# A two-layer hybrid decoder trunk: gate and up columns of its FFNs by seven half products per pair

## The chip, the cores and the metric

One program on one core of a Trainium2 chip. The metric is the device time of the program in microseconds (us). The kernel before took 2765.47 us, the median of three runs (2765.41 to 2768.8).

## The reference

The input x has 512 positions of 1024 features; everything is float32. Each of two layers runs an FFN, a token mixer (a gated DeltaNet and a dilated attention side by side) and a second FFN, each on a normalised and modulated copy of the residual:

```python
def modulate(x, shift, scale):
    return x * (1.0 + scale[:, None, :]) + shift[:, None, :]
def swiglu(x, w_gate, w_up, w_down):
    return (jax.nn.silu(x @ w_gate) * (x @ w_up)) @ w_down
for l in range(DEPTH):
    mod = c_act @ ada_w[l] + ada_b[l]
    (sh1, sc1, gt1, sh2, sc2, gt2, sh3, sc3, gt3) = jnp.split(mod, N_ADA, axis=-1)
    f = swiglu(modulate(rmsnorm(h, ln_ffn1[l]), sh1, sc1), ffn1_wg[l], ffn1_wu[l], ffn1_wd[l])
    h = h + MACARON_WEIGHT * gt1[:, None, :] * f
    u = modulate(rmsnorm(h, ln_mix[l]), sh2, sc2)
    m = hybrid_mixer(u, w_in[l], conv_w[l], a_log[l], dt_bias[l], dn_norm[l], w_a[l], w_b[l], w_o[l])
    h = h + gt2[:, None, :] * m
    f = swiglu(modulate(rmsnorm(h, ln_ffn2[l]), sh3, sc3), ffn2_wg[l], ffn2_wu[l], ffn2_wd[l])
    h = h + MACARON_WEIGHT * gt3[:, None, :] * f
return rmsnorm(h, final_norm)
```

The gate and up matrices are 1024 x 2816, the down matrix is 2816 x 1024. The change bears on `x @ w_gate` and `x @ w_up`, and on when `c_act @ ada_w` is computed.

## The kernel before, in words

The residual lies in SBUF as eight tiles `h` of 128 features x 512 positions. A product in full precision is made of three passes in a faster format (fp32r): each operand is split into a rounded high part and the rest, and high x high, low x high and high x low are summed in one PSUM bank. For a weight tile of 128 x 512 (four blocks of 128 x 128) the split is one copy on ACT (`wh`) and one subtraction on DVE (`wl`).

A gate or up matrix has 22 column blocks of 128. `dense` (line 298) makes one: 8 blocks along the 1024 features, 3 passes, so 24 matmuls of 128 x 512, each with its own 128 x 128 weights, into one bank. ACT then takes tanh of the gate bank, DVE forms the gated product with the up bank (`g`, `ay`), and `split` (line 739) halves it into `ah` and `al` for the down product. `ffn_order` (line 40) sets the order: the columns of a chunk of the 2816 inner features (`CHUNKS`, 8, 8 and 6 blocks), one ahead, and then the eight down columns over that chunk, whose banks DVE adds into `h`.

Every engine's queue is in the order in which this code is written; a wait in a queue holds all that stands behind it. Weights come from a list of `units`: `w_load` (line 242) issues the load on SP, `w_split` (line 254) the split, and `w_get` (line 277) sees to it that the split stands three units ahead of the one that PE is about to use:

```python
n = st["use"]
while st["split"] <= min(n + ahead, len(units) - 1):
    w_split()
```

The modulation vector is made on DVE, row block by row block, as 288 multiply-and-sum steps of 128 x 512 (`ada_step`, line 342; the tile is `ad`). They are dealt out by `tick`, which `mm_list` (line 288) calls after every third matmul: `ada["rate"]` says how many steps a tick issues, 0.42 in the FFNs until the last chunk. So all of layer 0 is made in its first FFN, and layer 1 in the second FFN of layer 0. GpSimd (POOL) is hardly used in an FFN.

At the end of each stage `tail` (line 481) finishes the last four columns in halves of 256 positions, makes the new normalised input `us` (high and low parts), and begins the first four weight units of the next stage, which for an FFN are gate and up of its first two blocks. `start` (line 633) does the same for the first FFN with eight units, four blocks.

## Time and profile before

| | |
|---|---|
| Median of three runs | 2765.47 us |
| Profiled execution: its own time | 2765.34 us |
| Profiled execution: span | 2763.6 us |
| PE busy | 2721.1 us, 98% |
| DVE busy | 1622.8 us, 59% |
| ACT busy | 1030.8 us, 37% |
| POOL busy | 496.8 us, 18% |
| Mean DMA rate | 126 GB/s |

The span is what the profiler recorded of one execution, from the first instruction to the last; the time of that execution is 1.7 us longer, and it is within 0.2 us of the median. The busy time of PE counts the matmuls with their modelled ends, which overlap, so the rate of PE is better read from the distance between starts. An average over the span hides that the stages differ: POOL's 18% lie nearly all in the two mixers and in the first 60 us.

### The profile page before, as it was taken

To read this page: it belongs to the slowest core of one execution; us is meant where nothing else is said; L and a number is where in the kernel's file an instruction comes from. 1 tells how busy PE (TensorE), PEld (TensorE's weight loads), DVE (VectorE), ACT (ScalarE), POOL (GpSimd) and SP (SyncE) were. 2 spreads that over 40 slices of the span, in tenths; PEclk is the share of its full clock that TensorE was granted. 3 is DMA by queue.
4 is the path that set the end of the run, shared out by engine and by line. 5 is a ranking of instruction groups with operands and counts; after the bars stand their busy time and mean duration, and the time that the engine had idled before them with its cause. 6 is when DMAs were issued, how large, how long until landed. Compare 5 with 4: busy or idle time off the path is not lost.

```text
span 2763.6 us, 39483 instructions
## 1 busy us (share of the span) xinstructions
PE 2721.1 (98%) x14812; PEld 2286.7 (83%) x14812; DVE 1622.8 (59%) x3325; ACT 1030.8 (37%) x2032; POOL 496.8 (18%) x965
## 2 busy tenths in 40 slices
PE   6999999999999999999999999999999999999998
PEld 4888888878888898888898888888788888988887
DVE  8877368666645467776454344776665454643435
ACT  4323235555533333222342222545554333432322
POOL 4000015353440000000010000254445100100001
PEclk9999999999999999999999999999999999999999
DMA  7776323442332337875323332324323333333332
GB/s 250 262 258 204 88 83 108 121 131 68 102 92 92 120 102 251 264 254 171 113 77 99 93 98 86 123 84 127 96 61 110 90 99 123 99 100 98 99 93 68
DMA packets 153391, 349.35 MB, mean 126 GB/s; under 512 B 41584, under 2 KB 44400, under 8 KB 153200
## 3 DMA queue, kind: packets, MB, share of 16 engines
q1 hardware_dynamic: 150640, 338.45, 39.4%
q0 software_dynamic: 2560, 8.39, 0.9%
q8 instruction: 116, 1.90, 0.3%
q14 instruction: 75, 0.61, 0.1%
HBM read 325.80 MB, written 11.53 MB: 122 GB/s over the span
## 4 chain that ended last, share of the span: by engine, by line
PE 93%; DVE 3%; DMA 1%; ACT 1%; issue 1%; SPq 1%; DVEq 0%; ACTq 0%
PE mm L117 80%; PE tl L117 4%; PE as L117 1%; PE ob L117 1%; PE pw L117 1%; PE pq L117 1%; PE po L117 1%; DVE wl L117 1%; PE aT L117 1%; DMA wr<-in_w_in_dram 1%; PE pm L117 1%; DVE sn L117 0%; DVE cy L117 0%; PE pt L117 0%; SPq L128 0%
## 5 line engine op out<-in xcount | busy, mean ns | idle before, releaser
L117 PE MATMUL mm<-uh,wh 128*128 128x512 f32 (+1 forms) x2608 | 680.9, 384 | 11.8 <-ACT uh L117 11.8
L117 PE MATMUL mm<-uh,wl 128*128 128x512 f32 (+1 forms) x2608 | 681.8, 382 | 0.0
L117 DVE TENSOR_TENSOR wl<-wr,wh 128x512 fp32r<-128x512 f32 (+1 forms) x904 | 597.4, 705 | 142.5 <-ACT wh L117 141.5
L117 PE MATMUL mm<-ul,wh 128*128 128x512 f32 (+1 forms) x2608 | 632.5, 380 | 1.6 <-DVE ul L117 1.6
L117 ACT ACTIVATE wh<-wr 128x512 fp32r<-128x512 f32 (+1 forms) x904 | 501.5, 609 | 253.6 <-DMA wr<-in_w_gu_dram 129.5
L117 PEld LDWEIGHTS mm<-uh,wh 128*128 128x128 f32 x2608 | 483.7, 189 | 104.0 <-ACT uh L117 16.8
L117 PEld LDWEIGHTS mm<-uh,wl 128*128 128x128 f32 x2608 | 487.1, 189 | 86.8 <-issue 0.7
L117 PEld LDWEIGHTS mm<-ul,wh 128*128 128x128 f32 x2608 | 466.6, 188 | 87.8 <-DVE ul L117 2.3
L117 POOL TENSOR_SCALAR y<-y,G,mod 128x256 f32<-128x256 f32 (+1 forms) x88 | 63.9, 728 | 1215.1 <-DVE y L117 1186.5
L117 ACT ACTIVATE ah<-ay 128x512 fp32r<-128x512 f32 x88 | 55.6, 632 | 380.6 <-DVE ay L117 380.6
L117 DVE SCALAR_TENSOR_TENSOR ad<-ad,ca 128x512 f32<-128x512 f32 x272 | 173.7, 689 | 0.0
L117 DVE SCALAR_TENSOR_TENSOR h<-mm,gt,h 128x512 f32<-128x512 f32 x88 | 65.2, 750 | 181.9 <-PE mm L117 181.9
L117 ACT ACTIVATE t<-mm 128x512 f32<-128x512 f32 x88 | 52.4, 595 | 315.8 <-PE mm L117 315.8
L117 DVE SCALAR_TENSOR_TENSOR g<-t,mm 128x512 f32<-128x512 f32 x88 | 60.4, 686 | 169.2 <-ACT t L117 169.2
L117 DVE TENSOR_TENSOR ay<-g,mm 128x512 f32<-128x512 f32 x88 | 60.4, 687 | 166.6 <-PE mm L117 165.6
L117 PE MATMUL mm<-ah,wl 128*128 128x512 f32 x608 | 152.8, 389 | 0.0
L117 PE MATMUL mm<-al,wh 128*128 128x512 f32 x608 | 152.7, 389 | 0.0
L117 PE MATMUL mm<-ah,wh 128*128 128x512 f32 x608 | 152.7, 389 | 0.0
L117 PEld LDWEIGHTS mm<-al,wh 128*128 128x128 f32 x608 | 114.1, 188 | 23.7
L117 PEld LDWEIGHTS mm<-ah,wl 128*128 128x128 f32 x608 | 114.1, 188 | 23.7
L117 PEld LDWEIGHTS mm<-ah,wh 128*128 128x128 f32 x608 | 114.1, 188 | 23.7
L117 DVE SCALAR_TENSOR_TENSOR cy<-mm,cw,cy 128x511 f32<-128x511 f32 x144 | 107.0, 746 | 7.0 <-ACT cy L117 3.6
(258 smaller groups left out, 2909.9 us busy)
## 6 DMA issues: line engine op xcount, KB each, us to landing
wr<-in_w_gu_dram SPq DMA_DIRECT2D x176, 512.0 KB, 3.7
ad<-in_ada_w_dram SPq DMA_DIRECT2D x288, 256.0 KB, 4.7
wr<-in_w_in_dram SPq DMA_DIRECT2D x132, 512.0 KB, 4.0
wr<-in_w_dn_dram SPq DMA_DIRECT2D x64, 512.0 KB, 3.6
wr<-in_w_dn_dram SPq DMA_DIRECT2D x32, 384.0 KB, 3.1
wr<-in_w_a_dram SPq DMA_DIRECT2D x16, 512.0 KB, 3.7
wr<-in_w_o_dram SPq DMA_DIRECT2D x16, 512.0 KB, 3.7
al<-in_alibi_dram SPq DMA_DIRECT2D x24, 256.0 KB, 3.2
```

Of the source, the lines that this page charges most:

```text
L117: return fn(*args, **kw)
```

## The change

From the first blocks on (four in the first FFN, two in the others), the gate and up columns are made in pairs. For a pair of column blocks the weights form a 2 x 2 matrix (two column blocks by two halves of the 1024 features, each quarter 128 x 512 in SBUF), and the input one of two halves of the features by two halves of the positions. `dense_pair` computes the 2 x 2 product by Strassen's way in Winograd's form: seven products of a quarter of weights (or a sum of quarters) and a quarter of the input (or a sum). Each product is 4 blocks x 3 passes, 12 matmuls of 128 x 256. In what follows a **round** is the seven products for one pair of blocks of either gate or up. There are 9 pairs in the first FFN and 10 in each of the others, so 78 rounds, and each stands where two `dense` calls stood, 48 matmuls of 128 x 512.

The products accumulate in three banks X, Y and Z. After each one, ACT copies the bank (products 0, 1, 2 and 6) or DVE adds it (3, 4 and 5) into the SBUF tiles `c1` and `c2`; X is written by products 0, 2, 4 and 6, so each of these follows the reading of the one before. Tanh and the gated product then read `c1` and `c2` from SBUF.

The four weight sums of a round are made on GpSimd (`w_sums`, tiles `ws0` to `ws3`, 128 x 512 each), and all seven quarters are split on ACT and DVE: seven splits a round where four were. The sums of the input are made once per FFN at the end of `tail` and `start` (`halves_sums`): 16 sums of 128 x 256, half on GpSimd and half on DVE, and 8 splits of 128 x 512.

Further: the split of weights stands 7 products (1.75 units) ahead of PE in an FFN; raw weights come as pieces of 256 KB out of the common pool of 84 buffers; there are four chunks, of 6, 6, 4 and 6 blocks; and the modulation steps run at 0.13 per tick, a tick being six matmuls in a round, with stops that leave 48 steps to each of the first three FFNs, 16 to the last, and 48 to each mixer (0.18 per tick, from the product that follows the attention).

```diff
-NBIG = 78
-CHUNKS = ((0, 8), (8, 16), (16, 22))
+NBIG = 84
+AHEAD = 1.75
+CHUNKS = ((0, 6), (6, 12), (12, 16), (16, 22))
...
-def ffn_order():
-    seq = []
-    gu = list(range(FF))
-    nxt = 0
+def ffn_order(first):
+    seq = [("gu", i) for i in range(first)]
+    nxt = first
     for ci, (lo, hi) in enumerate(CHUNKS):
-        ahead = min(hi + 1, FF)
-        while nxt < ahead:
-            seq.append(("gu", gu[nxt]))
-            nxt += 1
+        while nxt < min(hi + 1, FF):
+            seq.append(("pair", nxt))
+            nxt += 2
         seq.append(("down", ci))
     return seq
+def first_gu(l, f):
+    return 4 if (l, f) == (0, 0) else 2
...
+                elif kind == "pair":
+                    for gu in range(2):
+                        for j in (i, i + 1):
+                            units.append((("pair", l, f, j, gu), w_gu[l, f, j, gu], 8))
...
+    jobs = []
+    for n, u in enumerate(units):
+        if u[0][0] != "pair":
+            jobs.append((n, None))
+        elif u[0][3] % 2 == 0:
+            jobs += [(n, j) for j in range(7)]
+    st = {"load": 0, "split": 0, "use": 0, "ahead": 3, "lead": 0, "raw": 4}
...
+            raws[n] = []
+            for k0 in range(0, nk, 4):
+                m = min(4, nk - k0)
+                raws[n].append(big("wr", (128, m, 128)))
+                load(out=raws[n][-1], in_=src[:, k0:k0 + m])
         st["load"] += 1
...
+    def halves(r):
+        wh, wl = big("wh", (128, r.shape[1], 128), F32R), big("wl", (128, r.shape[1], 128), F32R)
+        A.activation(out=wh, in_=r, func=AF.Copy)
+        V.tensor_tensor(out=wl, in0=r, in1=wh.bitcast(F32), op=OP.subtract)
+        return wh, wl
+    def w_sums(n):
+        while st["load"] <= n + 1:
+            w_load()
+        (a11, a12), (a21, a22) = (raws[i] for i in (n, n + 1))
+        s1, s2, s3, s4 = (big(f"ws{i}", (128, 4, 128)) for i in range(4))
+        P.tensor_tensor(out=s1, in0=a21, in1=a22, op=OP.add)
+        P.tensor_tensor(out=s2, in0=s1, in1=a11, op=OP.subtract)
+        P.tensor_tensor(out=s3, in0=a11, in1=a21, op=OP.subtract)
+        P.tensor_tensor(out=s4, in0=a12, in1=s2, op=OP.subtract)
+        sums[n] = [s1, s2, s3, s4]
...
+        for n_, j_ in jobs[st["split"]:st["split"] + 4]:
+            if j_ == 0 and n_ not in sums:
+                w_sums(n_)
+        if j is not None:
+            if n not in sums:
+                w_sums(n)
+            s = sums[n]
+            src = (raws[n][0], s[0], s[1], raws[n][1], s[2], s[3], raws[n + 1][1])[j]
+            wh, wl = halves(src)
+            splits[n, j] = [(wh[:, k, :], wl[:, k, :]) for k in range(4)]
+            if j == 6:
+                raws.pop(n), raws.pop(n + 1), sums.pop(n)
+                w_fill()
...
+    def w_ahead(lead):
+        while st["split"] < len(jobs) and st["lead"] < lead:
+            w_split()
...
+        st["lead"] -= weight(job)
+        w_ahead(4 * ahead)
...
+    def dense_pair(keys, us, ts):
+        X, Y, Z = bank("mX"), bank("mY"), bank("mZ")
+        c1, c2 = big("c1"), big("c2")
+        lo, hi = HALF
+        def b(k0, sl):
+            return [(us[k][0][:, sl], us[k][1][:, sl]) for k in range(k0, k0 + 4)]
+        def copy(out, ps):
+            A.activation(out=out, in_=ps[:, lo], func=AF.Copy)
+        def add(out, ps):
+            V.tensor_tensor(out=out, in0=ps[:, lo], in1=out, op=OP.add)
+        for j, (ps, x, first, fn, out) in enumerate((
+                (X, b(0, lo), True, copy, c1[:, lo]), (Z, ts[0], True, copy, c2[:, hi]),
+                (X, ts[1], False, copy, c1[:, hi]), (Y, b(4, lo), True, add, c1[:, lo]),
+                (X, ts[2], False, add, c2[:, hi]), (Z, b(4, hi), False, add, c1[:, hi]),
+                (X, ts[3], False, copy, c2[:, lo]))):
+            w = w_get(keys[0], part=j)
+            lst = passes(w, x, range(4), lo)
+            mm_list([(ps[:, lo], a_, b_, first and i == 0, i == len(lst) - 1)
+                     for i, (a_, b_) in enumerate(lst)], 2 * Q)
+            fn(out, ps)
+        return c1, c2
...
+    def halves_sums(ys):
+        lo, hi = HALF
+        h12 = dnp.tile([128, 4, 2, 256], F32R, name=nm("th"), tag="MT")
+        l12 = dnp.tile([128, 4, 2, 256], F32R, name=nm("tl"), tag="W")
+        h34 = [dnp.tile([128, 2, 2, 256], F32R, name=nm("th"), tag=t_) for t_ in ("bt", "R")]
+        ts = [[None] * 4 for _ in range(4)]
+        for k in range(4):
+            E = (P, V)[k % 2]
+            a, b = big("ta", (128, 2, 256)), big("tb", (128, 2, 256))
+            y0, y1 = ys[k], ys[k + 4]
+            E.tensor_tensor(out=a[:, 0, :], in0=y0[:, hi], in1=y0[:, lo], op=OP.subtract)
+            E.tensor_tensor(out=a[:, 1, :], in0=y1[:, hi], in1=a[:, 0, :], op=OP.subtract)
+            E.tensor_tensor(out=b[:, 0, :], in0=y1[:, hi], in1=y0[:, hi], op=OP.subtract)
+            E.tensor_tensor(out=b[:, 1, :], in0=y1[:, lo], in1=a[:, 1, :], op=OP.subtract)
+            l34 = big("tl", (128, 2, 256), F32R)
+            for q, (t, th, tl) in enumerate(((a, h12[:, k], l12[:, k]), (b, h34[k // 2][:, k % 2], l34))):
+                A.activation(out=th, in_=t, func=AF.Copy)
+                V.tensor_tensor(out=tl, in0=t, in1=th.bitcast(F32), op=OP.subtract)
+                for i in range(2):
+                    ts[2 * q + i][k] = (th[:, i, :], tl[:, i, :])
+        return ts
...
+        w_ahead(12 if any(narrow) else 4)
+        ts = None if any(narrow) else halves_sums(yt)
...
+        w_ahead(4)
+        return us, pss, halves_sums(ys)
...
-        st["ahead"] = 3
-        ada["rate"] = 0.42
-        ada["stop"] = 144 if (l, f) == (0, 0) else len(ada_seq)
-        if f == 1 and ada["pos"] < ada["stop"]:
+        st.update(ahead=AHEAD, raw=4)
+        ada.update(rate=0.13, stop=min(len(ada_seq), 144 * l + 96 * f + 80))
...
+            elif kind == "pair":
+                g2s = dense_pair([("pair", l, f, j, 0) for j in (i, i + 1)], us, ts)
+                for c_ in g2s:
+                    t = big("t")
+                    A.activation(out=t, in_=c_, func=AF.Tanh, scale=0.5)
+                    V.scalar_tensor_tensor(out=c_, in0=t, scalar=1.0, in1=c_, op0=OP.add, op1=OP.mult)
+                ups = dense_pair([("pair", l, f, j, 1) for j in (i, i + 1)], us, ts)
+                for j, (c_, y) in enumerate(zip(g2s, ups)):
+                    V.tensor_tensor(out=y, in0=c_, in1=y, op=OP.mult)
+                    act[i + j] = split(y, "a")
...
-        st["ahead"] = 2
+        st.update(ahead=2, raw=3)
...
+        c_load()
+        c_silu()
+        ada.update(rate=0.18, stop=144 * l + 128)
...
```

Three places show how the instructions stand. The first is DVE's queue in the gate and up columns of the first FFN, before: `wl` is a weight split, `ad` a modulation step, `g`, `ay` and `al` the gated product and its low part, `mm` a PSUM bank.

```order
L117 TENSOR_TENSOR ay_939<-g_222_893,mm_905 128x512
L117 TENSOR_TENSOR al_942<-ay_939,ah_941 128x512
L117 TENSOR_TENSOR wl_946<-wr_903,wh_945 128x512
L117 TENSOR_TENSOR wl_950<-wr_903,wh_949 128x512
L117 SCALAR_TENSOR_TENSOR ad_915,acc_92<-ad_915,ca_108 128x512
L117 SCALAR_TENSOR_TENSOR ad_924,acc_92<-ad_924,ca_106 128x512
L117 SCALAR_TENSOR_TENSOR ad_933,acc_92<-ad_933,ca_108 128x512
L117 SCALAR_TENSOR_TENSOR g_245_991<-t_989,mm_955 128x512
L117 TENSOR_TENSOR wl_994<-wr_953,wh_993 128x512
L117 TENSOR_TENSOR wl_998<-wr_953,wh_997 128x512
L117 SCALAR_TENSOR_TENSOR ad_962,acc_92<-ad_962,ca_106 128x512
```

And DVE's queue now, in the second half of an up round of the first pair (`c_263` and `c_264` are `c1` and `c2` of the round, `mX`, `mY` and `mZ` its banks, `ws` a sum by GpSimd, `wr` a loaded quarter):

```order
L122 TENSOR_TENSOR wl_1063<-wr_839,wh_1062 128x512
L122 TENSOR_TENSOR c_263_998<-mY_996,c_263_998 128x256
L122 TENSOR_TENSOR wl_1080<-ws_240_898,wh_1079 128x512
L122 SCALAR_TENSOR_TENSOR ad_924,acc_92<-ad_924,ca_106 128x512
L122 TENSOR_TENSOR c_264_999<-mX_995,c_264_999 128x256
L122 TENSOR_TENSOR wl_1100<-ws_241_899,wh_1099 128x512
L122 TENSOR_TENSOR c_263_998<-mZ_997,c_263_998 128x256
L122 TENSOR_TENSOR wl_1117<-wr_843,wh_1116 128x512
L122 TENSOR_TENSOR c_263_998<-c_220_823,c_263_998 128x512
L122 TENSOR_TENSOR al_1143<-c_263_998,ah_1142 128x512
L122 TENSOR_TENSOR c_264_999<-c_221_824,c_264_999 128x512
L122 TENSOR_TENSOR al_1148<-c_264_999,ah_1147 128x512
```

Where two splits stood to one column, seven stand to a round, and three additions out of the banks stand between them; each addition waits for its product, and what follows it in the queue waits with it.

The second is ACT's queue, before, over one block:

```order
L117 ACTIVATE wh_2269<-wr_2226 128x512
L117 ACTIVATE wh_2273<-wr_2226 128x512
L117 ACTIVATE ah_2315<-ay_2313 128x512
L117 ACTIVATE wh_2319<-wr_2277 128x512
L117 ACTIVATE wh_2323<-wr_2277 128x512
L117 ACTIVATE t_2361<-mm_2329 128x512
L117 ACTIVATE wh_2365<-wr_2327 128x512
L117 ACTIVATE wh_2369<-wr_2327 128x512
L117 ACTIVATE ah_2404<-ay_2402 128x512
```

And now, from the end of an up round (`c_264<-mX_995`, the copy of its last product) into the next gate round, whose first copies are `c_296<-mX_1151` and `c_297<-mZ_1153`:

```order
L122 ACTIVATE wh_1099<-ws_241_899 128x512
L122 ACTIVATE wh_1116<-wr_843 128x512
L122 ACTIVATE c_264_999<-mX_995 128x256
L122 ACTIVATE ah_1142<-c_263_998 128x512
L122 ACTIVATE ah_1147<-c_264_999 128x512
L122 ACTIVATE wh_1156<-wr_968 128x512
L122 ACTIVATE c_296_1154<-mX_1151 128x256
L122 ACTIVATE wh_1173<-ws_272_1054 128x512
L122 ACTIVATE c_297_1155<-mZ_1153 128x256
L122 ACTIVATE wh_1193<-ws_273_1055 128x512
L122 ACTIVATE c_296_1154<-mX_1151 128x256
```

The copy of the next round's first product stands behind the two `ah`, which wait for DVE, and behind a weight split.

The third is GpSimd's queue, where nothing stood in this stage: the end of the input's sums, and the weight sums of two rounds.

```order
L122 TENSOR_TENSOR ta_758<-y_325 128x256
L122 TENSOR_TENSOR ta_758<-y_615,ta_758 128x256
L122 TENSOR_TENSOR tb_759<-y_615,y_325 128x256
L122 TENSOR_TENSOR tb_759<-y_615,ta_758 128x256
L122 TENSOR_TENSOR ws_238_896<-wr_841,wr_843 128x512
L122 TENSOR_TENSOR ws_239_897<-ws_238_896,wr_837 128x512
L122 TENSOR_TENSOR ws_240_898<-wr_837,wr_841 128x512
L122 TENSOR_TENSOR ws_241_899<-wr_839,ws_239_897 128x512
L122 TENSOR_TENSOR ws_272_1054<-wr_972,wr_974 128x512
L122 TENSOR_TENSOR ws_273_1055<-ws_272_1054,wr_968 128x512
```

They wait for no product of PE; each waits for its loaded quarters, for the sum before it and for a free buffer.

## Rows read from the trace of the kernel before

**Rows 1.** The page of the whole span: busy time by engine, and the granted clock.
```profile
span 2763.6 us, 39483 instructions
...
PE 2721.1 (98%) x14812; PEld 2286.7 (83%) x14812; DVE 1622.8 (59%) x3325; ACT 1030.8 (37%) x2032; POOL 496.8 (18%) x965
...
PEclk9999999999999999999999999999999999999999
```

**Rows 2.** The page, chain that ended last: shares of the span by engine.
```profile
PE 93%; DVE 3%; DMA 1%; ACT 1%; issue 1%; SPq 1%; DVEq 0%; ACTq 0%
```

**Rows 3.** Windows: busy us (x instructions) of PE, PEld, DVE, ACT, POOL; clock, DMA share, GB/s.
```profile
200.00:378.00 178.00, 178.00 (x787) 147.39 (x786) 97.08 (x200) 52.01 (x97) 0.00 (x0) 1.00 0.46 144
...
800.00:1000.00 200.00, 200.00 (x1182) 167.01 (x1181) 97.98 (x172) 68.97 (x130) 9.19 (x26) 1.00 0.37 114
```

**Rows 4.** Timeline of PE in a gate/up column: start us, us, operation, xcount.
```profile
205.08 1.98 PE L117 MATMUL mm<-uh,wh 128*128 128x512 f32 x8
...
212.34 1.98 PE L117 MATMUL mm<-uh,wl 128*128 128x512 f32 x8
```

**Rows 5.** Timeline of PE in a tail, where products have 256 columns.
```profile
1004.91 1.12 PE L117 MATMUL tl<-mh,wl 128*128 128x256 f32 x8
...
1010.67 1.12 PE L117 MATMUL tl<-mh,wl 128*128 128x256 f32 x8
```

**Rows 6.** Timeline of DVE in the same gate/up column as rows 4.
```profile
206.52 1.29 DVE L117 TENSOR_TENSOR wl<-wr,wh 128x512 fp32r<-128x512 f32 x2
...
208.33 0.69 DVE L117 SCALAR_TENSOR_TENSOR ad<-ad,ca 128x512 f32<-128x512 f32 x1
...
208.94 0.69 DVE L117 SCALAR_TENSOR_TENSOR ad<-ad,ca 128x512 f32<-128x512 f32 x1
```

**Rows 7.** Groups of DVE, 205 to 370 us, an FFN: busy us, mean ns | idle before, releaser.
```profile
L117 DVE TENSOR_TENSOR wl<-wr,wh 128x512 fp32r<-128x512 f32 x58 | 37.5, 684 | 0.0
L117 DVE SCALAR_TENSOR_TENSOR ad<-ad,ca 128x512 f32<-128x512 f32 x36 | 22.9, 685 | 0.0
L117 DVE TENSOR_TENSOR al<-ay,ah 128x512 fp32r<-128x512 f32 x11 | 7.6, 693 | 7.9 <-ACT ah L117 7.9
L117 DVE SCALAR_TENSOR_TENSOR h<-mm,gt,h 128x512 f32<-128x512 f32 x8 | 6.0, 750 | 26.6 <-PE mm L117 26.6
```

**Rows 8.** DVE on 256 elements out of PSUM (tile tl): min/median/max ns.
```profile
L117 DVE SCALAR_TENSOR_TENSOR h<-tl,gt,h x48: 475/484/485, 384.0 to 2751.7; 128x256 f32<-128x256 f32 x48
```

**Rows 9.** Groups of ACT, whole span.
```profile
L117 ACT ACTIVATE wh<-wr 128x512 fp32r<-128x512 f32 x856 | 488.1, 620 | 253.6 <-DMA wr<-in_w_gu_dram 129.5 <-DMA wr<-in_w_dn_dram 58.8 <-DMA wr<-in_w_b_dram 25.6
...
L117 ACT ACTIVATE ah<-ay 128x512 fp32r<-128x512 f32 x88 | 55.6, 632 | 380.6 <-DVE ay L117 380.6
L117 ACT ACTIVATE t<-mm 128x512 f32<-128x512 f32 x88 | 52.4, 595 | 315.8 <-PE mm L117 315.8
...
L117 ACT ACTIVATE PT<-aT 128x256 f32<-128x256 f32 x24 | 8.8, 366 | 0.2
```

**Rows 10.** Timeline of DVE and POOL side by side, both out of SBUF, at the start.
```profile
42.98 2.99 POOL L117 TENSOR_TENSOR ad<-ad,ca 128x512 f32<-128x512 f32 x2
43.09 1.73 DVE L117 TENSOR_TENSOR ul<-y,uh 128x512 fp32r<-128x512 f32 x1 [0.35 <-POOL y L117]
...
44.74 2.38 DVE L117 TENSOR_TENSOR wl<-wr,wh 128x512 fp32r<-128x512 f32 x2
...
47.04 0.68 DVE L117 SCALAR_TENSOR_TENSOR ad<-ad,ca 128x512 f32<-128x512 f32 x1
```

**Rows 11.** The same POOL operation over the run (tile ad): min/median/max ns.
```profile
L117 POOL TENSOR_TENSOR ad<-ad,ca x16: 1258/1666/1742, 13.2 to 64.4; 128x512 f32<-128x512 f32 x16
```

**Rows 12.** Timeline of DVE out of PSUM beside POOL, in the mixer.
```profile
464.78 1.49 POOL L117 TENSOR_TENSOR gu<-cm,gl 128x512 fp32r<-128x512 f32 x1
...
465.29 2.31 DVE L117 SCALAR_TENSOR_TENSOR cy<-mm,cw,cy 128x511 f32<-128x511 f32 x3
...
470.17 1.53 DVE L117 SCALAR_TENSOR_TENSOR cy<-mm,cw,cy 128x511 f32<-128x511 f32 x2
```

More of the change, by code (lines that the diff above doesn't have):

```diff
@@ L228, in trunk @@
                     units.append((("o", l, o), w_o[l, o], 8))
-            for kind, i in ffn_order():
+            for kind, i in ffn_order(first_gu(l, f)):
                 if kind == "gu":
@@ L237, in trunk @@
                                       w_dn[l, f, o][:, lo * 128:hi * 128], hi - lo))
-    NRAW = 3
-    st = {"load": 0, "split": 0, "use": 0, "ahead": 3}
-    raws, splits = {}, {}
+    jobs = []
[5 more added lines that the diff above has]
+    st = {"load": 0, "split": 0, "use": 0, "ahead": 3, "lead": 0, "raw": 4}
+    raws, splits, sums = {}, {}, {}
     def w_load():
@@ new lines, in w_load, with weight @@
+        st["load"] += 1
+    def weight(job):
+        return 4 if job[1] is None else 1
+    def halves(r):
[13 more added lines that the diff above has]
+        sums[n] = [s1, s2, s3, s4]
@@ L254, in w_split @@
     def w_split(load=True):
-        n = st["split"]
+        n, j = jobs[st["split"]]
+        st["split"] += 1
+        st["lead"] += weight((n, j))
         while st["load"] <= n:
             w_load()
+        for n_, j_ in jobs[st["split"]:st["split"] + 4]:
[11 more added lines that the diff above has]
+                w_fill()
+            return
@@ L260, in w_split, with w_fill, w_get, mm_list @@
         if units[n][0][0] == "in" and units[n][0][2] == T_BA:
-            splits[n] = r
-            st["split"] += 1
-            w_load()
-            return
-        parts = []
-        for k0 in range(0, nk, 4):
-            m = min(4, nk - k0)
-            wh, wl = big("wh", (128, m, 128), F32R), big("wl", (128, m, 128), F32R)
-            A.activation(out=wh, in_=r[:, k0:k0 + m], func=AF.Copy)
-            V.tensor_tensor(out=wl, in0=r[:, k0:k0 + m], in1=wh.bitcast(F32), op=OP.subtract)
-            parts.append((wh, wl))
-        splits[n] = [(parts[k // 4][0][:, k % 4, :], parts[k // 4][1][:, k % 4, :]) for k in range(nk)]
-        st["split"] += 1
-        if load:
-            w_load()
-    def w_get(key, ahead=None):
-        n = st["use"]
+            splits[n, None] = r
+            w_fill()
+            return
+        parts = [halves(x) for x in r]
+        splits[n, None] = [(parts[k // 4][0][:, k % 4, :], parts[k // 4][1][:, k % 4, :]) for k in range(nk)]
+        if load:
+            w_fill()
+    def w_fill():
+        while len(raws) < st["raw"] and st["load"] < len(units):
+            w_load()
+    def w_ahead(lead):
+        while st["split"] < len(jobs) and st["lead"] < lead:
+            w_split()
+    def w_get(key, ahead=None, part=None):
+        job = jobs[st["use"]]
         ahead = st["ahead"] if ahead is None else ahead
-        assert units[n][0] == key, (units[n][0], key)
-        while st["split"] <= min(n + ahead, len(units) - 1):
+        assert units[job[0]][0] == key and job[1] == part, (units[job[0]][0], key, job, part)
+        while st["split"] <= st["use"]:
+            if ahead < 0:
+                break
             w_split()
         st["use"] += 1
-        return splits.pop(n)
+        st["lead"] -= weight(job)
+        w_ahead(4 * ahead)
+        return splits.pop(job)
     Q = 3
-    def mm_list(lst):
+    def mm_list(lst, q=Q):
         for i, (ps, lhsT, rhs, start, stop) in enumerate(lst):
-            T.matmul(ps, lhsT=lhsT, rhs=rhs, start=start, stop=stop)
-            if i % Q == Q - 1:
+            T.matmul(ps, lhsT=lhsT, rhs=rhs, start=start, stop=stop, skip_group_check=q != Q)
+            if i % q == q - 1:
                 tick()
@@ L572, in tail @@
         ys = {}
+        yt = [big("y") for _ in range(NF)] if not any(narrow) else [None] * NF
         def first(k, hf):
@@ L625, in tail @@
         low()
-        while st["split"] < st["use"] + 3:
-            w_split()
+        w_ahead(12 if any(narrow) else 4)
+        ts = None if any(narrow) else halves_sums(yt)
         for k in range(NF):
@@ L733, in start @@
             V.tensor_tensor(out=sel, in0=sel, in1=ident[:, g:g + 16], op=OP.add)
-        w_load()
-        while st["split"] < st["use"] + 3:
-            w_split()
-        return us, pss
+        w_fill()
+        w_ahead(4)
+        return us, pss, halves_sums(ys)
     def split(y, s):
@@ L774, in ffn @@
                 last = i == len(CHUNKS) - 1
-                st["ahead"] = 4 if last else 3
+                st["ahead"] = 4 if last else AHEAD
                 if last:
@@ L794, in ffn, with mixer @@
         return tail([("dn", l, f, i, q) for q in range(NF - TAIL, NF)], xs, gt, nxt, Gs, adds)
-    def mixer(l, us, pss, nxt):
+    def mixer(l, us, pss, _, nxt):
         hd = {}
```

35 lines of the change are left out of this document (19 added, 16 removed).

## The prediction

> **What bounds the kernel now.** I read the page first: PE is busy for 2721.1 of 2763.6 us at a granted clock of 9 tenths or more in every slice [rows 1], and the chain that ended last is PE for 93% [rows 2]. Then the windows, since shares are averages: from 200 to 378 us, inside the first FFN, PE is busy all 178.00 us, with DVE at 97 [rows 3]. So the gate and up columns are PE-bound, and what the others do there is free as long as each keeps below PE's pace. That is the question of this change: it takes work from PE and gives more to DVE, ACT and GpSimd.
>
> **What PE gains.** In a gate/up column, 32 matmuls of 512 lie between starts at 205.08 and 212.34 us: 7.26/32 = 0.227 us each [rows 4]. In a tail, 48 matmuls of 256, each with its own weights, lie between 1004.91 and 1010.67: 0.120 us each [rows 5]; half the columns cost 53% of the time. A round replaces 48 of the first (10.89 us) by 84 of the second (10.08 us): 0.81 us gained, over 78 rounds **63 us**. The Trainium skill, TensorE: Matmul & The Clock Gate, section Back-to-back issue gap, gives N/2.4 + 2.5 ns for a matmul of N columns; by that a round would gain 1.19 us and the sum 93 us. The rows decide.
>
> **What DVE is given.** Back to back, a split of 128 x 512 takes 0.61 us (two in 1.29, one alone 0.684), and so does a modulation step (starts at 208.33 and 208.94) [rows 6, 7]. An addition of 256 out of PSUM lasts 0.484 [rows 8]; less the 0.07 that back-to-back operations overlap it is 0.42. A round now has:
> - 7 splits, 4.27 us; 3 additions, 1.26; 84/6 ticks at 0.13, so 1.82 modulation steps, 1.11.
> - A gate round: two `g` by 0.65, 1.3. They wait for the last copy and tanh: PE's last product starts when the addition of the fifth has freed bank X, takes 1.44, then a copy of 0.37 and a tanh of 0.60 [rows 9]. That is 2.4 us and some 0.25 of hand-overs (an estimate); in it DVE has two splits, an addition and a step to do, 2.25. So 0.4 is lost. Sum **8.4 us**.
> - An up round: `ay` and `al` for two blocks, 2.6, and each `al` stands right behind its `ay` and waits for ACT's `ah`, 7.9/11 = 0.72 us [rows 7], so 1.4 more. Sum **10.7 us**.
>
> Alone these would be just about PE's 10.08. But GpSimd makes four sums a round, and the trace shows what that does. At the start, DVE's `ul` and two `wl` beside two of GpSimd's `ad` (all out of SBUF) take from 43.09 to 47.04, 3.95 us where three take 1.83 [rows 10]: 1.06 us lost per GpSimd operation; `ul` lasts 1.73 instead of 0.684, and GpSimd's second operation runs long too, 1.74 at most against 1.258 alone [rows 11]. They take turns. Out of PSUM nothing is lost: three `cy` beside GpSimd's `gu` take 2.31, the same 0.78 a step as two later without it [rows 12]. The Trainium skill, SBUF — State Buffer, section Who interferes with whom, says that a DVE instruction with two SBUF inputs and a GpSimd one that reads SBUF exclude each other for the whole instruction; the rows agree. At a full 1.258 us per hit the sum below would be 62 x 3 x 0.2 = 37 us higher.
>
> All DVE operations of a round but the additions read two SBUF tiles. Of four GpSimd sums I take three as hits (the fourth falls under additions or waits): 3.2 us. So a gate round takes DVE **11.6 us**, an up round **13.9 us**, more than PE's 10.08. Can DVE lag? No: the additions stand in its queue between splits that serve PE seven products later, and product 6 waits for the addition of product 4. So PE gets at most one product, 1.44 us, ahead, and the split lead does not help. The round then goes at DVE's pace.
>
> **The rounds.** In the last up round of each of the 16 groups (four chunks in four FFNs) the splits ahead are those of down columns, and no sums are made: there PE's pace holds, 0.81 us gained. That leaves 39 gate and 23 up rounds:
> - gate: 39 x (11.6 - 10.89) = +27.7
> - up: 23 x (13.9 - 10.89) = +69.2
> - the last FFN has 16 modulation steps, so some 8 of its rounds lack 1.11 us: -8.9
> - 16 light rounds: -13.0
> - at each group's start PE may be 1.44 us ahead: 16 x 1.44 = -23.0
>
> **Entering an FFN.** Behind the last `ul`, DVE now has 4 splits, 8 sums of 256 and 8 splits (2.4 + 3.4 + 4.9 us) beside GpSimd's 4 weight sums and 8 halves (by 1.06 and about half of it: 8.5), so 19 us until the second product has its input. PE is covered by 64 + 32 tail products and product 0, (96 + 12) x 0.120 = 13 us. I take 7 us for each of three entries, and 10 at the start, where four blocks' gated products stand ahead of the first copy: **+31**.
>
> **At nothing** I cost: 32 more additions into `h` (0.750 us each, DVE, under down products), 32 more splits there, the 48 steps in each mixer (48 x 0.61 = 29 us on DVE, which is busy for 98 of 200 us there [rows 3]; uncovered, 59 us in all), and the halved loads (POOL and SP wait for none of it; DMA share 0.46 [rows 3]).
>
> Sum: 27.7 + 69.2 - 8.9 - 13.0 - 23.0 + 31 = +83. Against the profiled execution's 2765.34 us (0.1 under the median): **2848 us**, 3.0% slower.
>
> **Bounds.** Low: the hits fill all of DVE's waits and additions, so a round takes only the time in which SBUF reads exclude each other, 7.2 + 4 x 1.06 = 11.4 instead of a mean 12.45: -65, and entries at 15, -16: 2767. High: all four sums hit (+62), entries at 50: 2929. I take the middle, since a burst of four sums (4 x 1.7 = 7 us) must fall on DVE operations most of which read SBUF.
>
> **Rivals.**
> 1. *The sums hide* (slower, but little): rounds as in the low bound, entries as above, 2783. For it: DVE's waits at the end of an up round. Against it: GpSimd's queue waits for nothing of that round.
> 2. *PE-bound after all* (faster): GpSimd's queue runs ahead into the down products, where DVE idles, and its sums do not meet the rounds. Then gate rounds keep 10.08, but a place remains: after an up round ACT's queue has the two `ah` (a copy of 0.5, then `ah` 0.63, `al` and `ay` 1.3, `ah` 0.63: 3.1 us behind the last product), a split 0.6 and only then the copy of product 0, 4.1 us in all, while PE needs bank X after 2.88: 1.2 us, in 23 rounds, 28 us. So -63 + 28 + 20 for entries = -15: **2750 us**; without that place 2722. It decides when less than half a sum per round hits, (10.08 - 9.55)/1.06. For it: GpSimd waits only for loads and buffers. Against: only two units are loaded beyond the pair in hand, so it can lead by a round, not by a group.
> 3. *Worse*: with 84 buffers full, splits wait for buffers that PE frees late, on top of the above: 2930 or more.
> 4. *The pairs are not made*: excluded, the queue shows seven splits and three additions a round.
>
> **Numbers.** My case 0.55, rival 1 0.21, rival 2 0.14, rival 3 0.10. Own range 2800 to 2929. The range from **2755 to 2930** leaves out most of rival 2 and of 3. A difference under 0.2%, 5.5 us, cannot be told from none: faster 0.13 (rival 2), same 0.05 (between 1 and 2), slower 0.82.
>
> **What would show it.** PE busy well under 98%, with waits of `mX` for DVE's `c1`/`c2`; `wl` with a mean well over 0.684 us, and GpSimd's `ws` near 1.7; DVE busy in 9 tenths of the FFN's slices; rounds of 11.6 and 13.9 us; a gap of PE at each entry. If `wl` stays at 0.68 in the rounds, or PE has no gaps there, the forecast is wrong; if rounds are longer but PE waits for ACT's copies, its price is right by the wrong wait.

## The result, and the profile after

The changed kernel took 2912.62 us, the median of four runs (2911.05 to 2915.18), against 2767.03 for four runs of the kernel before, taken beside it: a ratio of 1.0527, 95% interval 1.0509 to 1.0545. It is slower by 5.3%; forecast were 2848 us, in a range from 2755 to 2930. The profiled execution took 2913.9 us, with a span of 2912.1.

The page of the changed kernel: busy time of each engine, then PE and its clock in the 40 slices, and the chain that ended last by engine.

```profile
PE 2712.7 (93%) x17620; PEld 2407.0 (83%) x17620; DVE 2166.7 (74%) x3929; ACT 1284.3 (44%) x2650; POOL 1016.0 (35%) x1309
...
PE   5789999999999996999979999999999999889998
...
PEclk9899999999999997999989999999999999989999
...
PE 77%; DVE 12%; ACT 4%; issue 3%; POOL 1%; DMA 0%; SPq 0%; DVEq 0%; ACTq 0%; POOLq 0%
```

PE was busy for 98% of the span, at a granted clock of 9 tenths or more in every slice [rows 1], and made 93% of the chain [rows 2]. Now it has holes in the first slices and in slices 16, 21, 35 and 36, where the FFNs begin, the clock dips in slices 2, 16, 21 and 36, and DVE holds 12% of the chain.

What PE waits for, from the view of waits (engine, what waits, what ended the wait: us in total, times, longest):

```profile
PE mX L122 <- ACT c L122: 78.8, 28, 8.6
PE mZ L122 <- ACT th L122: 35.2, 12, 6.3
PE mX L122 <- DVE c L122: 26.2, 22, 2.6
PE mm L122 <- ACT uh L122: 17.6, 9, 7.4
...
PE mX L122 <- DVE g L122: 9.2, 1, 9.2
```

In the kernel before, PE's longest wait was 12.5 us, for the squares of the first normalisation, and none of `mX`'s or `mZ`'s kind existed. The second row belongs to the entries of the three later FFNs: `th` is the split of the input's sums. The first is ACT's copy of product 0, at the four entries for 31 us and in other rounds for 48 us, 24 times.

The groups of DVE by shape over the whole span, which answer to [rows 7]:

```profile
L122 DVE TENSOR_TENSOR wl<-wr,wh 128x512 fp32r<-128x512 f32 x746 | 594.8, 820 | 119.9 <-ACT wh L122 118.8
L122 DVE TENSOR_TENSOR wl<-ws,wh 128x512 fp32r<-128x512 f32 x312 | 266.8, 871 | 9.4 <-ACT wh L122 7.7
L122 DVE SCALAR_TENSOR_TENSOR ad<-ad,ca 128x512 f32<-128x512 f32 x272 | 214.2, 801 | 0.1
```

`wl` is at 820 and 871 ns and `ad` at 801, where the kernel before has 720 and 689 as means over the program (684 and 685 in the FFN of [rows 7]). One round shows how. The timelines of DVE and of POOL in the first gate round of the second chunk (start us, us, operation):

```profile
189.52 1.78 DVE L122 TENSOR_TENSOR wl<-ws,wh 128x512 fp32r<-128x512 f32 x1
191.22 1.78 DVE L122 TENSOR_TENSOR wl<-wr,wh 128x512 fp32r<-128x512 f32 x1
192.93 0.41 DVE L122 TENSOR_TENSOR c<-mY,c 128x256 f32<-128x256 f32 x1
193.26 1.42 DVE L122 TENSOR_TENSOR wl<-ws,wh 128x512 fp32r<-128x512 f32 x1
```

```profile
190.71 1.75 POOL L122 TENSOR_TENSOR ws<-wr,wr 128x512 f32<-128x512 f32 x1
192.41 1.72 POOL L122 TENSOR_TENSOR ws<-wr,ws 128x512 f32<-128x512 f32 x1
```

A split takes 1.78 us beside a sum and the sum 1.75; the additions out of PSUM keep 0.41 beside the same sums, and a split after one of them is long again, 1.42. That is [rows 10] and [rows 12] again.

The starts of the rounds in that chunk, from the timeline of PE (the first product is the only one that reads `uh` into X):

```profile
184.62 0.64 PE L122 MATMUL mX<-uh,wh 128*128 128x256 f32 x4
...
196.60 0.64 PE L122 MATMUL mX<-uh,wh 128*128 128x256 f32 x4
...
207.94 0.64 PE L122 MATMUL mX<-uh,wh 128*128 128x256 f32 x4
...
215.92 1.22 PE L122 MATMUL mX<-th,wh 128*128 128x256 f32 x4 [4.95 <-ACT c L122]
...
225.16 0.64 PE L122 MATMUL mX<-uh,wh 128*128 128x256 f32 x4
```

Gate 11.98, up 11.34, gate 17.22 us, where PE alone needs 10.08. In the last of these PE waits 4.95 us for the copy of product 0, and the clock adds to it. PE was busy for 3.04 of the 7.98 us up to 215.92; the granted clock of the stretch behind is this (the numbers as in [rows 3]):

```profile
215.92:220.35 4.43, 4.43 (x20) 4.43 (x21) 2.40 (x4) 2.72 (x7) 0.00 (x0) 0.50 0.62 187
```

That is the lower of its two levels, and 24 matmuls take 4.43 us there where 24 x 0.120 = 2.88 is PE's pace. Read from PE's starts over all rounds, the matmuls that began at the lower level without a wait took 34 us more than at 0.120 us each, 13 us of it in the entries.

Read in the same way, the 78 rounds divide thus (a round ends where the next product begins; the excess is over the 10.89 us of the two columns that it replaces):

| | rounds | us in all | mean | excess measured | excess forecast |
|---|---|---|---|---|---|
| a network's first gate | 4 | 125.1 | 31.3 | +81.5 | +33.8 (with the entries' 31) |
| other gates | 35 | 442.3 | 12.6 | +61.1 | +24.9 |
| up | 23 | 248.9 | 10.8 | -1.6 | +69.2 |
| last up of a group | 16 | 161.2 | 10.1 | -13.0 | -13.0 |
| steps of the last FFN, group starts | | | | in the rows above | -31.9 |

Together +128.0 us of the 148.5 by which the span grew. Two waits of PE ahead of the very first pair (7.4 for `uh`, 9.2 for `g`) are 16.6 more. The remaining 4 us lie outside the rounds, most of them in the down products.

**An entry.** The windows of the second FFN's entry (busy us and count of PE, PEld, DVE, ACT, POOL; clock, DMA share, GB/s), then PE's timeline there and DVE's:

```profile
1090.00:1100.00 10.00, 4.28 (x30) 3.58 (x28) 8.53 (x9) 3.04 (x6) 9.41 (x10) 0.88 0.33 107
1100.00:1110.00 10.00, 2.87 (x10) 2.28 (x10) 9.94 (x13) 3.31 (x7) 4.64 (x3) 0.50 0.11 32
1110.00:1120.00 10.00, 3.27 (x15) 3.27 (x16) 7.06 (x12) 5.70 (x13) 0.00 (x0) 0.50 0.62 205
1120.00:1130.00 10.00, 10.00 (x80) 10.00 (x80) 8.89 (x12) 5.70 (x13) 6.33 (x4) 0.92 0.08 28
```

```profile
1106.89 0.58 PE L122 MATMUL mZ<-th,wh 128*128 128x256 f32 x1 [6.25 <-ACT th L122]
...
1116.73 1.22 PE L122 MATMUL mX<-th,wh 128*128 128x256 f32 x4 [7.55 <-ACT c L122]
...
1119.46 1.05 PE L122 MATMUL mY<-uh,wh 128*128 128x256 f32 x4
...
1121.17 0.80 PE L122 MATMUL mY<-ul,wh 128*128 128x256 f32 x4
```

```profile
1085.92 1.78 DVE L122 TENSOR_TENSOR wl<-wr,wh 128x512 fp32r<-128x512 f32 x1
...
1107.55 0.69 DVE L122 TENSOR_TENSOR tl<-tb,th 128x512 fp32r<-128x512 f32 x1
...
1114.37 0.69 DVE L122 TENSOR_TENSOR al<-ay,ah 128x512 fp32r<-128x512 f32 x1 [0.69 <-ACT ah L122]
```

The first product ran at 1091.71, the next round began at 1126.11: 34.4 us. PE's second product gets its last input at 1106.89, because DVE is at the splits of weights and of the input's sums until 1108.24. Behind them stand the reloaded `ca` and the gated products of the two blocks made earlier, up to 1115.06, and ACT's copy of product 0 stands behind their tanh and `ah` and behind four weight copies `wh`. So the third product starts at 1116.73. The granted clock has meanwhile fallen to 0.50, its lower level, and eight matmuls between 1119.46 and 1121.17 take 0.214 us each instead of 0.120.

### The profile page after: what moved, and what is told of

It is laid out like the page before. It is cut to its first block, busy times and chain, and to the rows that moved or that the text cites. A ratio compares the mean times of both kernels' runs of the same rounds, so it can differ in the third digit from the quotient of the medians.

```text
span 2912.1 us, 48690 instructions
## 1 busy us (share of the span) xinstructions
PE 2712.7 (93%) x17620; PEld 2407.0 (83%) x17620; DVE 2166.7 (74%) x3929; ACT 1284.3 (44%) x2650; POOL 1016.0 (35%) x1309
## 4 chain that ended last, share of the span: by engine, by line
PE 77%; DVE 12%; ACT 4%; issue 3%; POOL 1%; DMA 0%; SPq 0%; DVEq 0%; ACTq 0%; POOLq 0%
PE mm L122 45%; PE mX L122 11%; DVE wl L122 4%; PE mZ L122 4%; PE tl L122 4%; PE mY L122 3%; DVE c L122 3%; DVE ad L122 1%; ACT ah L122 1%; PE as L122 1%; ACT wh L122 1%; PE ob L122 1%; PE pw L122 1%; PE pq L122 1%; PE aT L122 1%
## 5 line engine op out<-in xcount | busy, mean ns | idle before, releaser
L122 DVE TENSOR_TENSOR wl<-wr,wh 128x512 fp32r<-128x512 f32 x858 | 654.0, 795 | 119.9 <-ACT wh L122 118.8
L122 ACT ACTIVATE wh<-wr 128x512 fp32r<-128x512 f32 x858 | 472.4, 592 | 141.7 <-PE mm L122 86.6
L122 POOL TENSOR_TENSOR ws<-wr,wr 128x512 f32<-128x512 f32 x156 | 246.0, 1577 | 825.9 <-DMA wr<-in_w_gu_dram 341.3
L122 PE MATMUL mm<-uh,wh 128*128 128x512 f32 (+1 forms) x1360 | 373.5, 379 | 17.6 <-ACT uh L122 17.6
L122 PE MATMUL mm<-uh,wl 128*128 128x512 f32 (+1 forms) x1360 | 373.6, 376 | 0.0
L122 PE MATMUL mm<-ul,wh 128*128 128x512 f32 (+1 forms) x1360 | 325.2, 373 | 1.6 <-DVE ul L122 1.6
L122 PEld LDWEIGHTS mm<-uh,wh 128*128 128x128 f32 x1360 | 249.6, 190 | 60.5 <-ACT uh L122 22.1
L122 PEld LDWEIGHTS mm<-uh,wl 128*128 128x128 f32 x1360 | 253.4, 190 | 38.6 <-issue 0.7
L122 DVE TENSOR_TENSOR wl<-ws,wh 128x512 fp32r<-128x512 f32 x312 | 266.8, 871 | 9.4 <-ACT wh L122 7.7
L122 PEld LDWEIGHTS mm<-ul,wh 128*128 128x128 f32 x1360 | 232.2, 189 | 39.0 <-DVE ul L122 2.3
L122 PE MATMUL mX<-th,wh 128*128 128x256 f32 x936 | 161.2, 296 | 105.0 <-ACT c L122 78.8
## 6 DMA issues: line engine op xcount, KB each, us to landing
wr<-in_w_dn_dram SPq DMA_DIRECT2D x96, 128.0 KB, 2.7
```

Of the source, the lines that this page charges most:

```text
L122: return fn(*args, **kw)
```

## The experiments

The theories at this point: **turns** (GpSimd's sums lengthen DVE's operations, and the rounds and entries pay for it), **queue order** (additions and copies come late only because of what is queued ahead of them), **load order** at the start, and for the entries too little **cover** on PE.

**Sums left out** (the products take the plain quarters in place of the sums):

```diff
-        P.tensor_tensor(out=s1, in0=a21, in1=a22, op=OP.add)
...
-        sums[n] = [s1, s2, s3, s4]
+        sums[n] = [a21, a22, a11, a12]
```

> The four weight sums of a round on GpSimd are left out (the raw quarters are split in their place, so the result is not the reference's); all else stands. Taking turns: beyond PE's pace the rounds after the first of an FFN cost 107 us in the changed kernel; without GpSimd only the wait at the end of an up round should stay (23 times 1.3 us, 30 us), and the four entries lose some 4 us each: 2912 - 77 - 16 = about 2820 us, with wl at 0.68 us in the rounds. Rival, queue order alone: the rounds are long because DVE and ACT have too much in their queues, GpSimd or not: 2900 us or more.

2796.97 us, 115.6 below the change and 23 below what was expected; against before 1.0108 (1.0071 to 1.0145). Its engines, its first group of DVE by shape, and its largest wait:

```profile
PE 2679.8 (96%) x17620; PEld 2381.9 (85%) x17620; DVE 1941.3 (69%) x3929; ACT 1280.8 (46%) x2650; POOL 534.6 (19%) x997
```

```profile
L122 DVE TENSOR_TENSOR wl<-wr,wh 128x512 fp32r<-128x512 f32 x1058 | 739.2, 724 | 155.5 <-ACT wh L122 151.2
```

```profile
PE mX L122 <- ACT c L122: 54.9, 27, 7.8
```

`wl` is back at 724 ns (720 before the change), and PE's waits for DVE's `c` are gone. DVE's busy time fell by 2166.7 - 1941.3 = 225 us for 312 sums: 0.72 us a sum, two thirds of the 1.06 lost in a full hit. The time fell by 0.37 us a sum, less than DVE's loss; that the rest falls into DVE's slack is argued. Some 22 of the 115.6 us are PE's clock: read as above, the matmuls at the lower level now cost 12 us instead of 34, all of it at the entries. Turns are shown, and a rival that leaving out the sums would also remove, splits that wait for a sum made late, is not there: in the changed kernel ACT's `wh` waits for GpSimd's sums for 0.4 us in all. Two things remain without sums: entries (1061.78 to 1087.09 for a first round, 25.3 us), and 1.2 us in each gate round behind an up round (1097.16 to 1108.45 is 11.29, the up round before it 10.07).

**Sums twice** (each of the four made a second time into the same tile):

```diff
+        for o, x0, x1 in ((s1, a21, a22), (s2, s1, a11), (s3, a11, a21), (s4, a12, s2)):
+            P.tensor_tensor(out=o, in0=x0, in1=x1, op=OP.add if o is s1 else OP.subtract)
```

> GpSimd makes each weight sum twice, into the same tile. Taking turns: four more operations a round, of which three hit at 1.06 us, in 62 rounds, and four at each entry: about 2912 + 200 + 16 = 3130 us. Queue order alone, or GpSimd running ahead in gaps: within 25 us of 2912.

3149.84 us in its one run, 237 above the change. The waits, and the busy time in five rounds of the second FFN (numbers as in [rows 3]):

```profile
PE mX L122 <- DVE c L122: 181.2, 37, 8.6
```

```profile
1297.00:1380.00 83.00, 58.37 (x420) 57.11 (x419) 77.17 (x91) 28.67 (x61) 57.46 (x35) 0.86 0.32 104
```

The second set costs 0.76 us a sum, twice the first. DVE is busy for 77 of these 83 us, so little slack is left, and the wait is now its addition; 52 of the 237 us are matmuls at the lower clock. GpSimd is busy for 57 of the 83 us, and over the whole program ACT's `wh` waits for its sums for 12 us, so it is no bound itself. The Trainium skill, SBUF — State Buffer, section Who interferes with whom, describes the path shared by DVE and GpSimd as an exclusive lock; the lengthened `wl` and `ws`, and the unchanged additions out of PSUM, agree.

**A longer cover** (two more blocks by eight products ahead of each network's first pair, and their splits further ahead):

```diff
-    return 4 if (l, f) == (0, 0) else 2
+    return 6 if (l, f) == (0, 0) else 4
...
-        w_ahead(12 if any(narrow) else 4)
+        w_ahead(12 if any(narrow) else 16)
```

> Each FFN makes two more blocks by dense products before its first pair (six in the first FFN, four in the others), with four weight units split ahead of the input's sums, so that PE has some 22 us of work while the sums are made. Entry by queue order: the first rounds fall from 34 (22 in the first FFN) to about 12 us, four times, less 8 rounds' gain of 0.81: 2912 - 78 + 6 = about 2840 us. Rival: DVE is short of time over the whole FFN, and the work shifted off the entry is waited for in the rounds behind it: no lower than 2885 us.

2867.33 us, 45 below the change and 27 above what was expected, between the two cases. The starts of the first two rounds of the second FFN:

```profile
1104.05 1.23 PE L122 MATMUL mX<-uh,wh 128*128 128x256 f32 x4 [4.72 <-ACT wh L122]
...
1125.14 0.64 PE L122 MATMUL mX<-uh,wh 128*128 128x256 f32 x4
```

The first round fell from 34.4 to 21.1 us, not to 12 (in the first FFN it fell from 22.5 to 10.1). DVE only reaches the pair's splits later, since the gated products of four blocks instead of two are queued among them.

**Gated products handed over** (issued behind the third product of the next gate round, so that the copy of product 0 no longer stands behind them):

```diff
+                late_acts.append(acts)
...
+            if j == 2:
+                flush()
```

> The gated product and the split of a pair's two blocks are issued after the third product of the next round instead of ahead of it, and both products ahead of both splits; all else stands. Taking turns: only the wait at the end of an up round goes, 23 times 1.3 us: about 2882 us, with rounds that still wait for DVE. Queue order alone: most of the 107 us that the rounds lose goes: 2830 us or less.

2879.53 us, 33 below. The waits:

```profile
PE mX L122 <- DVE c L122: 51.3, 42, 3.3
...
PE mX L122 <- ACT c L122: 34.8, 7, 8.6
```

The waits for ACT fell from 78.8 to 34.8 (mostly the entries' share), those for DVE rose from 26.2 to 51.3. Queue order is worth 33 us, as the first case said, and does not restore PE's pace: with turns in force, another operation is late.

**Load order at the start** (the look-ahead for sums begins only when the first stage is set up):

```diff
-            if j_ == 0 and n_ not in sums:
+            if j_ == 0 and n_ not in sums and st["peek"]:
```

> The changed kernel, with the look-ahead of the weight sums' loads kept short at the very start of the program, so that the first pieces of the modulation weights are asked for ahead of them. Theory (the loads pulled forward at the start delay the first modulation step by one): TensorE's 7.35 us wait at 42 to 49.6 us goes, the time is some 6 to 7 us below the change, about 2906 us. Rival (the first stage is bound by VectorE there, whichever loads come first): within 2 us of 2912.

2913.44 us (ratio to before 1.0541, 1.0523 to 1.0558): no difference from the change. My theory fell, the rival held:

```profile
PE mX L122 <- DVE g L122: 14.1, 1, 14.1
```

The wait of 7.4 for `uh` is gone, and the one before the first pair grew from 9.2 to 14.1. A delay removed ahead of a queue that is full anyway comes back at its end.

**The three edits together.**

> Three edits together: a larger cover of down products ahead of each feed-forward network's first pairs, the weight sums of a step issued ahead of its other work, and the start's loads in their old order. If the gains of the three add up (45 and 33 us measured one at a time, 7 expected), about 2827 us. If two of them remove the same waits, 2845 or more.

The three are the longer cover, the gated products handed over and the load order; the sums are issued where they were, other than the words above say. 2836.61 us (1.0262, 1.0241 to 1.0283), between the two cases. With the start's loads worth nothing, 45 and 33 us make 2834: they add up.

**Modulation steps only beside down products** (0.4 a tick there, none beside pairs):

```diff
-        ada.update(rate=0.13, stop=min(len(ada_seq), 144 * l + 96 * f + 80))
+        ada.update(rate=0.0, stop=min(len(ada_seq), 144 * l + 96 * f + 80))
...
+                ada["rate"] = 0.0 if last else ADADN
```

> The three edits, and the modulation steps issued only beside down products, where VectorE has room, none beside pairs. By taking turns and VectorE's load, the heavy rounds lose what the modulation adds cost there: about 20 to 30 us below the run with the three edits, about 2800 us. If the down products' own waits take their place (VectorE late with their h), nothing is gained.

2856.02 us, 19 above the run before, so a miss. The timeline of DVE behind the second FFN's first pairs:

```profile
1160.21 0.69 DVE L123 SCALAR_TENSOR_TENSOR ad<-ad,ca 128x512 f32<-128x512 f32 x1
...
1169.40 0.68 DVE L123 SCALAR_TENSOR_TENSOR ad<-ad,ca 128x512 f32<-128x512 f32 x1
...
1193.81 1.78 DVE L123 SCALAR_TENSOR_TENSOR ad<-ad,ca 128x512 f32<-128x512 f32 x1
```

The first down products need the gate `gt`, whose last 16 steps had not been made, so all 16 stand in one piece in DVE's queue; then come two to three steps a down column, some at 1.78. DVE reaches the next pair's additions late, and the round behind takes 18.8 us.

**Shorter groups** (in addition, the lines below; also the weights beside the blocks by eight products are split 3.75 units ahead, and the last of these blocks is split for the down product only behind the first pair's third product):

```diff
-CHUNKS = ((0, 6), (6, 12), (12, 16), (16, 22))
+CHUNKS = ((0, 4), (4, 8), (8, 12), (12, 16), (16, 22))
```

> As the run before, and the pairs in shorter groups: two pairs, then the down products of four blocks, with the inputs of a network's first pairs split further ahead. By the theory that the heavy rounds are slow because GpSimd's sums fall into them, a queue of sums made during the down products serves a group of two without slowing it: 30 to 60 us below the run before, 2740 to 2770 us, level with the kernel before the change or below it. Rival (the sums cost VectorE as much wherever they run): within 10 us of the run before.

2915.38 us (1.0549, 1.0533 to 1.0565), 59 above the run before: neither theory gave this. The wait that is new:

```profile
PE mm L123 <- DVE wl L123: 56.8, 17, 15.8
```

A wait that was 1.3 us in the changed kernel is now 56.8: the shorter down products end before DVE has split their weights. That GpSimd's work cannot be parked there because DVE's own backlog is there already is how I read it. Which of the three edits weighs most was not separated.

**Pairs behind the first down products only** (eight blocks of each network by eight products, the modulation steps and the input's sums beside them, the other 14 blocks in pairs without steps; with the hand-over and the load order of above):

```diff
-    return 4 if (l, f) == (0, 0) else 2
+    return 8
...
-        ts = None if any(narrow) else halves_sums(yt)
+        ts = None if any(narrow) else lambda: halves_sums(yt)
...
+                if i == 2:
+                    ts = ts()
```

> Pairs only where the runs so far show them to pay: the first eight blocks of each feed-forward network are made by eight products as in the kernel before, the modulation steps all stand beside these blocks and the first down products, the input's sums are made beside them too, and the other 14 blocks are made in pairs, without modulation steps. By the theory that the change lost its time at the entries and through VectorE's turns with GpSimd plus the steps, no entry is left, and these 14 rounds cost what they cost in the last network of the run with the three edits (62.9 + 41.1 + 43.0 us where eight products take 14 x 10.89 = 152.5): 5.5 us gained in each of four networks, about 2743 us, below the kernel before. Rival (the pairs' rounds are held up by GpSimd's sums whatever else VectorE has to do): 2765 us or more.

2762.28 us, 0.9992 of before (0.9983 to 1.0002): 19 short of the forecast, but the entries are gone, and no difference from before is clear. The 56 rounds take 40 us more than PE's pace; the largest piece is one round:

```profile
158.18 0.64 PE L122 MATMUL mX<-uh,wh 128*128 128x256 f32 x4
...
182.73 0.88 PE L122 MATMUL mX<-uh,wh 128*128 128x256 f32 x4
```

In the first network 24.6 us. Ahead of it DVE has two to three modulation steps in each down column, some of 1.77 us, as in the run with steps beside down products. Most of the rest lies in the 16 gate rounds behind an up round, 1.0 us over PE's pace in the mean.

**Sums issued earlier** (`st["split"] + 4` becomes `+ 7`).

> The run before it, with GpSimd's sums of a pair issued seven splits ahead of their use instead of four. If the rounds behind down products still wait for sums that come late, 2 to 8 us below that run; if what they wait for is VectorE taking turns with GpSimd, no difference over 3 us.

2767.18 us (1.0014, 1.0004 to 1.0024), 5 above. The first gate round of each last group fell from 11.9 or 12.1 to 10.1 or 10.5 us; but up rounds elsewhere rose (11.7 to 16.4 in the second network's first group), where the sums now met other operations of DVE. The sums had not been late: in the run before, ACT's `wh` waits for them for 0.2 us in all. They ran beside that gate round's splits; issued earlier, they run beside others. So the turns moved, and nothing is gained.

**Fewer steps beside down products** (0.2 a tick beside all of them but a network's last, where the first ones alone had 0.42):

```diff
+                ada["rate"] = 0.0 if last else 0.2
```

> The run with pairs behind the first down products, with the modulation steps beside all down products but a network's last at less than half the rate (0.2 instead of 0.42 a tick). Its first pairs of the first network took 24.6 us, 14.5 over TensorE's pace, because VectorE had three steps a down column, some of them at 1.7 us beside GpSimd's sums, and reached the pair's first addition late. If that lag is the steps' doing, this round falls to 10 to 13 us and the time is about 2750 us; if it is the sums' doing, the round stays above 20 and the time within 3 us of 2762.

2749.94 us, 0.9948 (0.9934 to 0.9961). The same two starts:

```profile
157.93 0.64 PE L122 MATMUL mX<-uh,wh 128*128 128x256 f32 x4
...
169.07 0.64 PE L122 MATMUL mX<-uh,wh 128*128 128x256 f32 x4
```

11.1 us instead of 24.6. The lag was the steps' doing.

**Gated products in three portions** (behind products 2, 4 and 5):

```diff
-            if j == 2:
-                flush()
+            if j in (2, 4, 5) and late_acts:
+                late_acts.pop(0)()
```

> The run with fewer steps in the down products, and the gated products of a pair handed to VectorE in three portions (behind products 2, 4 and 5 of the next gate round) instead of one. If the 0.8 us by which a gate round behind an up round exceeds TensorE's pace (10.9 against 10.1, 16 times) comes from additions that stand behind these four operations, 8 to 13 us less than that run, about 2740 us; if it comes from ScalarE's queue, no change.

2738.17 us, 0.9904 (0.9891 to 0.9918): 1% below the kernel before, the best version here. Its page, its largest wait for DVE's additions, and three starts in the second FFN:

```profile
PE 2681.7 (98%) x16828; PEld 2346.6 (86%) x16828; DVE 2024.6 (74%) x3797; ACT 1217.6 (45%) x2496; POOL 886.5 (32%) x1221
```

```profile
PE mX L122 <- DVE c L122: 9.5, 7, 1.6
```

```profile
1157.70 0.64 PE L122 MATMUL mX<-uh,wh 128*128 128x256 f32 x4
...
1167.83 0.64 PE L122 MATMUL mX<-uh,wh 128*128 128x256 f32 x4
...
1177.91 0.64 PE L122 MATMUL mX<-uh,wh 128*128 128x256 f32 x4
```

These two rounds take 10.1 us each, and so do all 16 gate rounds behind an up round, so the additions were the cause. 56 rounds by 0.81 would give 45 us; the span fell by 2763.6 - 2736.0 = 27.6. Another 13 us are still lost in rounds: the first gate round of each network's last group takes 11.9 us, and an up round that no down product follows 10.35 in the mean. DVE's share of the span is that of the changed kernel (74%, with 56 rounds in place of 78): much of what differs is when.

## Why the prediction was right and wrong

**Right: the direction and its cause.** PE's gain is there wherever nothing else holds it: a light round takes 10.1 us, the forecast's 10.08. The formula that the prediction quotes from the Trainium skill, TensorE: Matmul & The Clock Gate, section Back-to-back issue gap, is given there for an isolated matmul; by it 84 matmuls would take 9.2 us, an estimate, and no round here does. DVE's turns with GpSimd eat the gain: 115.6 us come back when the sums go. The assumed hits, three sums of four, were near: 0.72 us of DVE's time lost per sum is 0.68 of 1.06.

**The rounds: right in sum, wrong in their parts.** Forecast for gate and up rounds were 24.9 + 69.2 - 31.9 = +62.2; measured are 61.1 - 1.6 = +59.5. That these agree is partly luck. But the up round's 13.9 us was 10.8, and the gate round's 11.6 was 12.6. The working booked the gated products under the up round; they stand behind its last product, so their cost falls into the next gate round. And the sign that was to show it, `mX` waiting for DVE's additions, was the smaller part: 26.2 us against 78.8 for ACT's copy. This is the place of rival 2, the copy behind the two `ah`, made longer by the sums: 2.0 us in the mean outside the entries and 4.95 at 215.92, instead of its 1.2. Without sums it is just that 1.2. By the prediction's own sign, its price is then right by the wrong wait. And it has no term for the clock, which costs some 21 us in the rounds behind the entries; without the sums it costs nothing there.

**Wrong: the term "Entering an FFN", +31.** The first rounds' 81.5 us and the start's 16.6 make 98, against 33.8 with their share of the gate rounds: 64 us short, nearly the whole miss (+83 was forecast, the span grew by 148.5). DVE's part in it was priced about right: from the last `ul` (1085.92) to the second product's last input (1106.89) it is 21.0 us, where 19 were forecast. Three things make "I take 7 us" too small. The cover is 7.2 us, not 13: the first product ends at 1093.15, since 48 of the 64 tail products ran while DVE was still at the `ul`. So the second product has its last input 13.7 us after the first is done, not 6. The chain behind it, gated products of earlier blocks and then the copy of product 0, was seen at the start and not counted at the three other entries; at the second FFN it is 7.55 us of PE's wait. And the lower clock stretches what follows, by 13 us in the four first rounds. A longer cover alone made the kernel 45 us faster; with no pairs there the entries are gone.

**At nothing.** The 48 steps in each mixer cost nothing: from 840 to 1040 us, inside the first mixer, PE is busy for all of it and DVE for 126 us against 98 in [rows 3], which is the 29 us of the steps.

```profile
840.00:1040.00 200.00, 200.00 (x1182) 167.05 (x1181) 126.30 (x262) 69.61 (x132) 18.24 (x35) 1.00 0.57 182
```

The additions into `h` and the splits under the down products cost little: between the groups the down products took 351.8 us, where the pace of the kernel before (43.52 us for eight blocks) gives 348.2. The loads drawn forward leave a wait of 7.4 us at the start, and taking that away gained nothing.

**Rivals.** 1 and 2 fell, since the sums neither hide nor run ahead. The pairs are made. Rival 3's buffer waits were not looked into by a run of their own, but the trace speaks against them. Splits do wait for PE, which I take for a wait for a buffer:

```profile
ACT wh L122 <- PE mm L122: 100.2, 61, 3.7
```

All of it falls outside the rounds, and PE's waits for a split there are 1.3 us.

## What to carry to other kernels

Work taken from TensorE and given to the engines that feed it pays only where these have room at that moment: ask at each place what VectorE has queued, above all where a stage begins and every operand is made anew. An elementwise operation moved to GpSimd is not free for VectorE when both read SBUF (here 0.72 us of VectorE for each 128 x 512 sum). Using the cheaper form in part, behind work that covers its inputs, and spreading what stands in one piece in a queue together turned 5.3% slower into 1% faster with the same arithmetic per pair.

## What was not expected of the hardware

- TensorE's clock fell to its lower level (1.2 of 2.4 GHz) in a gap that it spent waiting on others: the granted clock was 0.88 from 1090 to 1100 us, with PE busy for 4.28 of 10 us, and 0.50 in the next two windows, with 2.87 and 3.27. It was back at 0.92 in the window in which PE was busy throughout. A single wait of 4.95 us within a round also ended at 0.50, with 24 matmuls in 4.43 us behind it instead of 2.88. Waits cost more than their length.
- The first sums per round cost PE 0.37 us each, a second set 0.76, of which 0.17 is the lower clock: contention is cheaper while DVE has slack.
- A modulation step on DVE, a multiply with a running sum, is lengthened beside a GpSimd sum as a split is, to 1.78 us (at 1193.81 in the run with steps beside down products) from 0.68.
